# First Strassen pair's weight sums issued ahead of the norm, and the spatial norm's weight and bias applied after the mixing product

## The chip, the cores and the metric

The kernel runs on 1 core of a Trainium2 chip. The metric is device time in microseconds (us) of one execution. The engines are named as the profile names them: PE (TensorE matmul), PEld (its weight load), DVE (VectorE), ACT (ScalarE), POOL (GpSimd), SP (SyncE, which issues DMAs). Each engine takes its instructions in the order in which they were issued to it; an instruction that waits for a semaphore holds all that stand behind it on the same engine.

## The reference

One inference step of a model of two layers on 576 tokens (512 of a prompt, 64 new ones), width 1024, all in float32. Layer 0 mixes tokens with attention and a gated recurrence, layer 1 with chunked spatial gating; behind each mixer stands a gated feed-forward network (FFN) of inner width 2816 with a short causal convolution. After each of these four parts comes `x = layer_norm(alpha * x + f(x))`. What the change touches of it:

```
def layer_norm(x, g, b):
    mu = mean(x); var = mean((x - mu)**2)
    return (x - mu) * rsqrt(var + eps) * g + b

def odd_mixer(x, ...):                      # layer 1
    u, v = split(gelu(x @ w_in), 2)
    v = layer_norm(v, sgu_g, sgu_b)         # over the 1024 channels of a token
    ...
    v = sum over s <= t of sgu_w[group, t, s] * v[s] + sgu_bias[group, t]
    return (u * v) @ w_out                  # chunks of 128 tokens, 8 groups of 128 channels
```

The normalised v of the 64 new tokens is also an output of its own (output 14).

## The kernel before, in words

**Number format.** A float32 product is made of three passes of TensorE on a value's high part and low part: `xh*whi`, `xl*whi`, `xh*wlo` (a triplet, L419 to L421). A weight tile `raw` is split on the chip: ACT copies it into `whi` with rounding (L307), DVE subtracts `raw - whi` into `wlo` (L308). The residual stream is `x`, with channels on the partitions, in two halves of 288 tokens.

**FFN.** Function `ffn` makes the up-projection from 11 blocks of channel pairs. Blocks 0 and 1 are plain. From block 2 on, each is a Strassen pair: 7 products in place of 8, for which sums of token halves of x (`x_sums`, L1364 to L1381) and sums of weight halves are needed. The weight work of a pair (`pair_weights`) is: high and low part of two raw tiles; four sums of 128x512 on POOL, in place on the raw tiles, called s1, s3 (on the second tile) and s2, s4 (on the first) (L1263 to L1267); for each of the two summed tiles two ACT copies (L1276, L1277) and a DMA from POOL's queue (L1278) that adds the raw tile onto the negated high part, which gives the low part. A planner (class `Plan`, L70) puts this work, with costs and due times, into the queues; when a raw tile is used up, the load of a later unit is issued on SP (L1230).

**Start of an FFN.** At an FFN's start the norm of the residual is only half done. The first products, of the first token half (`sweep(us, 0, ...)`), run on PE while the second half ("half 1") is normalised by hooks that the sweep calls after so many of its steps: at step 13 `stats` (sums by PE at L554, a few small DVE instructions, the power on POOL at L564), at 15 `center` (mean spread by PE transposes at L571 into a PSUM bank; ACT copies it into `cs`, L578; 5 subtractions on DVE at L581, 3 on POOL at L583), at 17 and 20 `scale` (per channel block k: DVE L591, then ACT makes `xh` at L593, POOL the scaled x at L594, DVE `xl` at L603). At step 2 the hook `begin` (L1538 to L1541) splits the first Strassen pair's two plain operands. The rest of that pair's weight work is given to the planner behind the sweep, by `pair_weights(g2, begun=True)`. Then PE does the second token half of blocks 0 and 1 (`plain_second`, L1211 in the trace, as are all products of the planner), which needs `xh` and `xl` of half 1 for one k after the other.

**Spatial gating.** v is computed token-major by `v_sweep` (L824 to L826) into `vo` (four tiles of 128 tokens, one of 64, 1024 channels wide). Then DVE takes statistics (L1671, L1672), POOL the power (L1674), ACT normalises the five tiles (L1678), and each tile is multiplied by `gB` (DVE, L1679) and gets `bB` added (POOL for tiles 0 to 2, DVE for 3 and the sample tile 4, L1680). Meanwhile PE computes three of the u units (4, 5, 6; L419 to L421). Next `mix_sample` multiplies the sample tile by the masked spatial weights `wsT` (L1688), DVE adds the spatial bias `sB` (L1689), and `mix(g)` does the same for one group of the prompt (L1694, L1696) and multiplies by u (L1698); mixes 0 and 1 come at once, mix 2 between the halves of u unit 7, mixes 3 to 7 inside the loop over k of the output projection, whose products need their results `hh` (ACT, L1700) and `hl` (DVE, L1707). The mixing products have plain float32 operands, and the trace shows two records for each matmul of the code. `psmain` holds 6 PSUM banks named `mm` and 2 named `aux`; `auxbank()` hands out the two `aux` banks in turn, and the next user of a bank waits until the last reader of it is done.

Of the kernel before, what the change touches and what calls it, by code (L numbers as in the profile page):

```python
# [19 lines left out]
FT = mybir.dt.float32  # L20
# [5 lines left out]
D = 1024  # L26
# [145 lines left out]
def stream_step(ctx, tc, I, O):  # L172
# [44 lines left out]
    def weight_list():  # L217
        w = I["w_in_e"]
        E = {}
        col = {"q": 0, "k": 512, "xb": 1544, "gb": 2056}  # L220
        for name in ("xb0", "xb1", "xb2", "xb3", "gb0", "gb1", "gb2", "gb3"):
            E[name] = wunit(w, 0, EC, col[name[:2]] + 128 * int(name[2]), 0, 8, "A")
        E["v"] = [vunit(w, EC, 1024, 2 * i, "A", 520) for i in range(4)]
        for name in ("q0", "k0", "q1", "k1", "q2", "k2", "q3", "k3"):
            E[name] = wunit(w, 0, EC, col[name[:-1]] + 128 * int(name[-1]), 0, 8, "A")
        E["out"] = [wunit(I["w_out_e"], 0, D, 128 * m, 0, 8, "A") for m in range(8)]
        Fs = []

        def ffn_units(layer):
            up, down = {}, {}  # L230
            w = I["ffn_w_up"]

            def src(j, s, slot):
                return (w, layer * D * 2 * DFF, 2 * DFF, s * DFF + 128 * j, 0, 8, slot)

            for j in range(2):
                up[j] = [wunit(*src(j, s, "B")) for s in range(2)]
            tmp = [Unit(None, None, 0) for _ in range(2)]
            units.extend(tmp)
            for j in range(2, NJ):  # L240
                up[j] = wpair(wsrc(*src(j, 0, None)), wsrc(*src(j, 1, None)), j)
            for c, (j0, j1) in enumerate(CHUNKS):
                for m in range(8):
                    u = down[c, m] = wsrc(I["ffn_w_down"], layer * DFF * D, D, 128 * m, j0, j1 - j0, None)
                    u.slots = [j % RING for j in range(j0, j1)]
                    if c == len(CHUNKS) - 1:
                        units.append(u)
            Fs.append((up, down, tmp))

        ffn_units(0)  # L250
        w = I["w_in_o"]
        Od = {}
        Od["u"] = {}
        for m in range(4):
            Od["u"][m] = wunit(w, 0, 2 * D, 128 * m, 0, 8, "A")
        Od["v"] = [[vunit(w, 2 * D, D + 512 * s, 2 * i, "A") for i in range(4)] for s in range(2)]
        for m in range(4, 8):
            Od["u"][m] = wunit(w, 0, 2 * D, 128 * m, 0, 8, "A")
        Od["out"] = [wunit(I["w_out_o"], 0, D, 128 * m, 0, 8, "A") for m in range(8)]
        ffn_units(1)  # L260
        return E, Fs, Od

# [207 lines left out]
    class Norm:  # L470
# [100 lines left out]
                PE.transpose(bk[:, t:t + n], self.st[half][:n, c + j:c + j + 1].to_broadcast([n, 128]), ident[:n, :n])  # L571
            return bk[:, :b - a]

        def center(self, half):
            a, b = self.halves[half]
            mu = self.spread(half, 0)
            ms = self.cs[half]
            ACT.activation(ms, mu, AF.Copy)  # L578
            for k in range(8):
                if k < 5:  # L580
                    DVE.tensor_sub(x[:, k, a:b], x[:, k, a:b], mu)  # L581
                else:
                    POOL.tensor_sub(x[:, k, a:b], x[:, k, a:b], ms)  # L583
# [592 lines left out]
    def ffn(layer, prev, norm):  # L1176
# [68 lines left out]
        def sl(j, q):  # L1245
            return ("S", j % 2, q, "h", 0), ("S", j % 2, q, "h", 1), ("S", j % 2, q, "l", 0), ("S", j % 2, q, "l", 1)

        def pair_weights(g, begun=False):
            j = g.j
            r1, r2 = rres(g.one), rres(g.two)  # L1250
            R = lambda e, c: (g.one if e == 1 else g.two).raw[:, c]
# [1 line left out]
            h0, h1, l0, l1 = sl(j, 0)  # L1253
            k0, _, m0, _ = sl(j, 1)
            al = slice(0, 1024)
            if not begun:
                plan.add("ACT", 1.05, lambda: ACT.activation(W(0)[0][:, al], R(1, al), AF.Copy), r1, (h0, h1), tag=f"a1hi{j}")
                plan.add("DVE", 1.22, lambda: DVE.tensor_sub(W(0)[1][:, al], R(1, al), W(0)[0][:, al]), r1 + (h0, h1),
                         (l0, l1), True, tag=f"a1lo{j}")
                plan.add("ACT", 0.62, lambda: ACT.activation(W(1)[0][:, a_], R(2, b_), AF.Copy), r2[1:], (k0,), tag=f"a2hi{j}")  # L1260
                plan.add("DVE", 0.69, lambda: DVE.tensor_sub(W(1)[1][:, a_], R(2, b_), W(1)[0][:, a_]), (r2[1], k0),  # L1261
                         (m0,), True, tag=f"a2lo{j}")
            plan.add("POOL", 1.3, lambda: POOL.tensor_add(R(2, b_), R(2, a_), R(2, b_)), r2, r2[1:], True, tag=f"s1_{j}")  # L1263
            plan.add("POOL", 1.3, lambda: POOL.tensor_sub(R(2, a_), R(1, a_), R(2, a_)), (r1[0], r2[0]), r2[:1], True, tag=f"s3_{j}")
            split_sums(g, 2, r2)
# [274 lines left out]
            DVE.tensor_sub(l2[:, a_], g2.two.raw[:, b_], h2[:, a_])  # L1540
            DVE.tensor_sub(l1[:, :1024], g2.one.raw[:, :1024], h1[:, :1024])  # L1541

        hooks[2] = begin
        sweep(us, 0, xh, xl, g_first, outer=True, hooks=hooks)
        retire(us)
        close_ln()
# [1 line left out]
        sum_tiles(tp)  # L1548
        loaded["dma"], loaded["freed"] = st["dma"], st["freed"]
        x_sums()  # L1550
        pair_weights(g2, begun=True)
        d_next()
        plain_second(0)
        base(0, 1)
# [77 lines left out]

    first_group([Od["u"][m] for m in range(4)], u_post, n2)
    vo = op.tile([128, 5, D], FT, name="vo")
    gB = op.tile([128, D], FT, name="gB")
    bB = op.tile([128, D], FT, name="bB")
    sB = op.tile([128, 8, 128], FT, name="sB")
    wsr = op.tile([128, 8, 128], FT, name="wsr")
    wsT = op.tile([128, 8, 128], FT, name="wsT")
    nc.sync.dma_start(wsr, dram(I["sgu_w"], 0, [[128, 128], [128 * 128, 8], [1, 128]]))  # L1640
    nc.sync.dma_start(gB, dram(I["sgu_g"], 0, [[0, 128], [1, D]]))
    nc.sync.dma_start(bB, dram(I["sgu_b"], 0, [[0, 128], [1, D]]))
    nc.sync.dma_start(sB, dram(I["sgu_bias"], 0, [[0, 128], [128, 8], [1, 128]]))
    up_mask = op.tile([128, 128], FT, name="up_mask")
    jo = op.tile([128, 128], I32, name="jo")
    POOL.iota(jo, pattern=[[1, 128]], base=0, channel_multiplier=-1)
# [26 lines left out]
    DVE.tensor_scalar(rsv, mv[:, :, 1], EPS, None, op0=OP.add)  # L1673
    POOL.tensor_tensor(rsv, rsv, nhalf[:, 0:5], op=OP.pow)  # L1674
    DVE.scalar_tensor_tensor(mv[:, :, 0], mv[:, :, 0], -1.0, rsv, op0=OP.mult, op1=OP.mult)
    for t in range(5):
        n = 128 if t < 4 else TS
        ACT.activation(vo[:n, t], vo[:n, t], AF.Identity, scale=rsv[:n, t:t + 1], bias=mv[:n, t, 0:1])  # L1678
        DVE.tensor_mul(vo[:n, t], vo[:n, t], gB[:n])  # L1679
        (POOL if t < 3 else DVE).tensor_add(vo[:n, t], vo[:n, t], bB[:n])  # L1680
    nc.sync.dma_start(dram(O[14], 0, [[D, TS], [1, D]]), vo[:TS, 4])

    ms = op.tile([128, 8, TS], FT, name="ms")

    def mix_sample():
        bk = mmbank().rearrange("p (g t) -> p g t", g=8)
        for g in range(8):
            PE.matmul(bk[:, g], vo[:TS, 4, 128 * g:128 * g + 128], wsT[:TS, g, :TS], start=True, stop=True)  # L1688
        DVE.tensor_add(ms, bk, sB[:, :, :TS])  # L1689

    def mix(g):
        bk = auxbank()
        for t in range(4):
            PE.matmul(bk[:, 128 * t:128 * t + 128], vo[:, t, 128 * g:128 * g + 128], wsT[:, g, :], start=True, stop=True)  # L1694
        mt = op.tile([128, T], FT, name="mt", bufs=3)
        DVE.tensor_add(mt[:, :TP].rearrange("p (n t) -> p n t", n=4), bk.rearrange("p (n t) -> p n t", n=4),  # L1696
                       sB[:, g, None, :].to_broadcast([128, 4, 128]))
        DVE.tensor_mul(mt[:, :TP], mt[:, :TP], x[:, g, :TP])  # L1698
        POOL.tensor_mul(mt[:, TP:], ms[:, g], x[:, g, TP:])
        ACT.activation(hh[:, g, :], mt, AF.Copy)  # L1700
        mts[g] = mt
        mix_low(g - 1)
        POOL.tensor_add(x[:, g, :], xh[:, g, :].bitcast(FT), xl[:, g, :].bitcast(FT))
# [174 lines left out]
```

## Time and profile before

| | us |
|---|---|
| median of 3 runs | 1285.21 |
| lowest and highest run | 1285.07, 1285.76 |
| the profiled execution's own time | 1287.51 |
| its span, first to last instruction | 1285.5 |

The rows further down come from the one profiled execution. A row of the timeline gives start, duration, engine, line, operation and tiles; "x8" joins 8 instructions of a kind, and the brackets name the engine's idle time before it and what ended it. PE is busy for 96% of the span, DVE 79%, ACT 52%, POOL 46%; the mean granted clock of TensorE is 0.985 of full speed. Times in the kernel's course, in us of the span: layer 0's mixer to about 265, its FFN to about 660, layer 1's mixer to about 860, its FFN to the end.

### The profile page before, as it was taken

What the parts mean: (1) busy time and instruction counts of PE and PEld (TensorE: products, weight loads), DVE (VectorE), ACT (ScalarE), POOL (GpSimd) and SP (SyncE); (2) the same over time, 40 slices, a digit from 0 to 9 for tenths busy, and PEclk for the clock granted to TensorE, in tenths of its full rate; (3) what the DMA queues carried; (4) which work ended last, traced back from release to release, by engine and by line L of the source; (5) the groups of instructions that cost most, each with busy time, mean ns of one, the idle gap of its engine ahead of it and who ended that gap; (6) DMA issues with size and microseconds to landing.
All of it is one profiled execution on the core that took longest, in us unless ns stands there. A gap on an engine that the chain in (4) does not pass through costs nothing.

```text
span 1285.5 us, 23770 instructions
## 1 busy us (share of the span) xinstructions
PE 1238.7 (96%) x9111; PEld 1198.7 (93%) x9111; DVE 1010.2 (79%) x1874; ACT 664.6 (52%) x1062; POOL 592.6 (46%) x650
## 2 busy tenths in 40 slices
PE   8999999998999999999999998999899999999995
PEld 7999887998999999999989788998899999999995
DVE  4647686789998899878875238888899898888877
ACT  4553554348655656556444233347565556655542
POOL 3223132486455556555054005765645546555313
PEclk9999999999999999999989998999999999999998
DMA  8415320306755768766521422214657667956512
GB/s 224 133 34 164 100 92 27 104 1 146 177 138 146 168 144 195 162 143 144 144 69 38 160 66 62 63 54 100 141 121 179 147 144 178 196 127 162 134 47 75
DMA packets 204566, 155.78 MB, mean 121 GB/s; under 512 B 6524, under 2 KB 187036, under 8 KB 204452
## 3 DMA queue, kind: packets, MB, share of 16 engines
q1 hardware_dynamic: 192324, 111.96, 30.2%
q0 software_dynamic: 12128, 42.30, 18.5%
q8 instruction: 72, 1.18, 0.4%
q14 instruction: 42, 0.34, 0.1%
HBM read 107.07 MB, written 5.22 MB: 87 GB/s over the span
## 4 chain that ended last, share of the span: by engine, by line
PE 70%; DVE 13%; issue 9%; ACT 3%; POOL 3%; DMA 2%; DVEq 0%; SPq 0%; POOLq 0%; ACTq 0%
PE mm L1211 33%; PE aux L1211 17%; PE mm L419 4%; PE mm L420 4%; PE mm L421 4%; POOL x L594 2%; DMA wloB<-raw 1%; DVE raw L1364 1%; DVE wloA L308 1%; PE o L1103 1%; PE aux L554 1%; DVE vo L1679 1%; DMA raw<-in_w_in_e_dram 1%; ACT whiA L307 1%; PE mm L772 1%
## 5 line engine op out<-in xcount | busy, mean ns | idle before, releaser
L1324 DVE SCALAR_TENSOR_TENSOR y<-hb,vecF,y 128x578 f32<-128x578 f32 x176 | 166.3, 974 | 4.8 <-ACT y L1314 3.4
L308 DVE TENSOR_TENSOR wloA<-raw,whiA 128x1024 fp32r<-128x1024 f32 (+2 forms) x54 | 65.6, 1232 | 97.3 <-ACT whiA L307 97.3
L1211 PE MATMUL mm<-xh,wloB 128*128 128x288 f32 x384 | 113.4, 295 | 0.0
L1211 PE MATMUL mm<-xl,whiB 128*128 128x288 f32 x384 | 113.4, 295 | 0.0
L1211 PE MATMUL mm<-xh,whiB 128*128 128x288 f32 x384 | 113.4, 295 | 0.0
L419 PE MATMUL mm<-xh,whiA 128*128 128x288 f32 (+2 forms) x320 | 96.5, 302 | 3.9 <-ACT xh L650 3.9
L1211 PE MATMUL mm<-xh,whiA 128*128 128x288 f32 x320 | 94.8, 296 | 5.2 <-ACT xh L1379 3.6
L1263 POOL TENSOR_TENSOR raw<-raw 128x512 f32<-128x512 f32 x40 | 59.2, 1479 | 87.0 <-DVE wloA L1261 35.9
L421 PE MATMUL mm<-xh,wloA 128*128 128x288 f32 (+2 forms) x320 | 95.0, 297 | 1.5 <-DVE wloA L308 1.5
L1211 PE MATMUL mm<-xl,whiA 128*128 128x288 f32 x320 | 94.9, 297 | 1.0 <-DVE xl L1381 1.0
L420 PE MATMUL mm<-xl,whiA 128*128 128x288 f32 (+2 forms) x320 | 95.3, 298 | 0.4 <-DVE xl L651 0.4
L1338 POOL COPY stage<-hb 128x4 f32<-128x4 f32 x88 | 50.8, 677 | 95.5 <-DVE hb L1483 69.8
L1211 PE MATMUL mm<-xh,wloA 128*128 128x288 f32 x320 | 94.5, 295 | 0.0
L1447 DVE TENSOR_TENSOR x<-x,aux 128x288 f32<-128x288 f32 x160 | 71.4, 448 | 23.5 <-PE aux L1211 22.4
L1314 ACT ACTIVATE y<-hb,vecF 128x578 f32<-128x578 f32 x88 | 74.5, 864 | 29.5 <-DVE hb L1483 20.7
L307 ACT ACTIVATE whiA<-raw 128x1024 fp32r<-128x1024 f32 (+2 forms) x54 | 54.4, 1022 | 62.5 <-PE mm L826 44.4
L1211 PE MATMUL aux<-hh,wloA 128*128 128x288 f32 x272 | 80.8, 297 | 1.5 <-DVE wloA L1422 1.5
L1211 PE MATMUL aux<-hh,whiA 128*128 128x288 f32 x272 | 81.1, 298 | 0.2
L1211 PE MATMUL aux<-hl,whiA 128*128 128x288 f32 x272 | 80.8, 297 | 0.0
L1211 PE MATMUL aux<-hl,whiB 128*128 128x288 f32 x272 | 80.4, 296 | 0.0
L1211 PE MATMUL aux<-hh,wloB 128*128 128x288 f32 x272 | 80.4, 295 | 0.0
L1211 PE MATMUL aux<-hh,whiB 128*128 128x288 f32 x272 | 80.3, 295 | 0.0
(435 smaller groups left out, 4682.0 us busy)
## 6 DMA issues: line engine op xcount, KB each, us to landing
raw<-in_ffn_w_up_dram SPq DMA_DIRECT2D x88, 512.0 KB
wloA<-raw POOLq DMA_DIRECT2D x40, 512.0 KB, 5.0
wloB<-raw POOLq DMA_DIRECT2D x40, 512.0 KB, 4.9
draw<-in_ffn_w_down_dram SPq DMA_DIRECT2D x80, 192.0 KB
raw<-in_w_in_o_dram SPq DMA_DIRECT2D x16, 512.0 KB
raw<-in_w_in_e_dram SPq DMA_DIRECT2D x14, 512.0 KB
raw<-in_ffn_w_down_dram SPq DMA_DIRECT2D x16, 320.0 KB
raw<-in_w_out_e_dram SPq DMA_DIRECT2D x8, 512.0 KB
```

The lines of the kernel that those rows point to most:

```text
L307: ACT.activation(u.hi[:, c], u.raw[:, c], AF.Copy)
L308: DVE.tensor_sub(u.lo[:, c], u.raw[:, c], u.hi[:, c])
L419: PE.matmul(o, wh, h[:, k, a:b], start=first, stop=False)
L420: PE.matmul(o, wh, l[:, k, a:b], start=False, stop=False)
L421: PE.matmul(o, wl, h[:, k, a:b], start=False, stop=last)
L594: POOL.tensor_scalar(xk, xk, g, bb, op0=OP.mult, op1=OP.add)
L1211: PE.matmul(bank[key][:, :w], lhs(), rhs(), start=first, stop=stop)
L1263: plan.add("POOL", 1.3, lambda: POOL.tensor_add(R(2, b_), R(2, a_), R(2, b_)), r2, r2[1:], True, tag=f"s1_{j}")
L1314: plan.add("ACT", 0.86, lambda: ACT.activation(y, t[:, 2:580], AF.Identity, scale=V[:, 88 + ct:89 + ct], bias=V[:, 132 + ct:133 + ct]), hr ...
L1324: plan.add("DVE", 0.82, lambda q=q, y=y, t=t, ct=ct: DVE.scalar_tensor_tensor(y, t[:, q:q + 578], V[:, 44 * q + ct:44 * q + ct + 1], y, op ...
L1338: plan.add("POOL", 0.4, lambda s=s, t=t: POOL.tensor_copy(stage[:, :, s * NJ + j].rearrange("p (a b) -> p a b", a=2), t[:, 448:580].rearra ...
L1447: DVE.tensor_add(xm, xm, bank[key][:, :H2])
```

## The change

**Part one, both FFNs.** The first Strassen pair's sums, high parts and accumulating DMAs leave the planner and become hooks of the sweep, written out by hand: at step 3 the sums s1 and s3, at 6 the two ACT copies of the second tile (`parts(2)`), at 13 the stats, then the second tile's DMA (`rest(2)`) and the sums s2 and s4, at 15 the centre, now with all 8 subtractions on DVE, then `parts(3)`, `rest(3)` and the release of both raw tiles. In the list of loads, the two empty units that stand for the temporary buffers move from ahead of pair 2 to behind it, so that the next pair's raw tiles are asked for earlier.

**Part two, spatial gating.** `vo` stays without g and b, but for the sample tile's copy that goes to output 14. g and b come as 16 rows of 128 (`gbr`), a PE transpose makes columns of them, which DVE copies into `gbc` (b times 1024). Since g and b belong to a channel and the mixing sums over tokens, b's share of the result is b times the column sum of `wsT`: two matmuls with a column of 1/1024 give these sums, and 8 DVE instructions add them, times b, to `sB`. g is applied where the bias is added.

```diff
@@ load order
             tmp = [Unit(None, None, 0) for _ in range(2)]
-            units.extend(tmp)
             for j in range(2, NJ):
                 up[j] = wpair(wsrc(*src(j, 0, None)), wsrc(*src(j, 1, None)), j)
+                if j == 2:
+                    units.extend(tmp)
@@ Norm.center
-        def center(self, half):
+        def center(self, half, on_vector=5):
...
-                if k < 5:
+                if k < on_vector:
@@ ffn
-        hooks[2] = begin
+        def sums(q):
+            r1, r2 = g2.one.raw, g2.two.raw
+            if q == 2:
+                POOL.tensor_add(r2[:, b_], r2[:, a_], r2[:, b_])
+                POOL.tensor_sub(r2[:, a_], r1[:, a_], r2[:, a_])
+            else:
+                POOL.tensor_sub(r1[:, a_], r2[:, b_], r1[:, a_])
+                POOL.tensor_sub(r1[:, b_], r1[:, b_], r1[:, a_])
+
+        def parts(q):
+            hi, lo = (t[:, :1024] for t in S[0][q])
+            r = (g2.two if q == 2 else g2.one).raw[:, :1024]
+            ACT.activation(hi, r, AF.Copy)
+            ACT.activation(lo, r, AF.Copy, scale=-1.0)
+
+        def rest(q):
+            POOL.dma_start(S[0][q][1][:, :1024], (g2.two if q == 2 else g2.one).raw[:, :1024], accum_op=OP.add)
+
+        def middle():
+            prev.stats(1)
+            rest(2)
+            sums(3)
+
+        def end():
+            prev.center(1, 8)
+            parts(3)
+            rest(3)
+            free_raw(2)
+
+        hooks.update({2: begin, 3: lambda: sums(2), 6: lambda: parts(2), 13: middle, 15: end})
         sweep(us, 0, xh, xl, g_first, outer=True, hooks=hooks)
...
         x_sums()
-        pair_weights(g2, begun=True)
         d_next()
@@ spatial gating
-    for t in range(5):
+    for t in (4, 0, 1, 2, 3):
         n = 128 if t < 4 else TS
         ACT.activation(vo[:n, t], vo[:n, t], AF.Identity, scale=rsv[:n, t:t + 1], bias=mv[:n, t, 0:1])
-        DVE.tensor_mul(vo[:n, t], vo[:n, t], gB[:n])
-        (POOL if t < 3 else DVE).tensor_add(vo[:n, t], vo[:n, t], bB[:n])
-    nc.sync.dma_start(dram(O[14], 0, [[D, TS], [1, D]]), vo[:TS, 4])
+    DVE.tensor_mul(gB, vo[:TS, 4], gB)
+    DVE.tensor_add(gB, gB, bB)
+    nc.sync.dma_start(dram(O[14], 0, [[D, TS], [1, D]]), gB)
+    bk = auxbank()
+    PE.transpose(bk[:, :16], gbr, ident[:16, :16])
+    DVE.tensor_copy(gbc[:, 0:8], bk[:, 0:8])
+    DVE.tensor_scalar(gbc[:, 8:16], bk[:, 8:16], float(D), None, op0=OP.mult)
+    for g0 in (0, 4):
+        bk = auxbank()
+        PE.matmul(bk, mone[:, 0:1].to_broadcast([128, 128]), wsT[:, g0:g0 + 4].rearrange("p g t -> p (g t)"),
+                  start=True, stop=True)
+        for g in range(4):
+            DVE.scalar_tensor_tensor(sB[:, g0 + g], bk[:, 128 * g:128 * g + 128], gbc[:, 8 + g0 + g:9 + g0 + g], sB[:, g0 + g],
+                                     op0=OP.mult, op1=OP.add)
...
-        DVE.tensor_add(ms, bk, sB[:, :, :TS])
+        DVE.tensor_mul(ms, bk, gbc[:, 0:8, None].to_broadcast([128, 8, TS]))
+        DVE.tensor_add(ms, ms, sB[:, :, :TS])
...
-        DVE.tensor_add(mt[:, :TP].rearrange("p (n t) -> p n t", n=4), bk.rearrange("p (n t) -> p n t", n=4),
-                       sB[:, g, None, :].to_broadcast([128, 4, 128]))
+        DVE.scalar_tensor_tensor(mt[:, :TP].rearrange("p (n t) -> p n t", n=4), bk.rearrange("p (n t) -> p n t", n=4),
+                                 gbc[:, g:g + 1], sB[:, g, None, :].to_broadcast([128, 4, 128]), op0=OP.mult, op1=OP.add)
```

How instructions move on the engines, at the places that matter (names with A or B are the tiles' buffers).

PE in the changed kernel, right behind the last product of `v_sweep` (L827), with the semaphores that an instruction waits for; `mone` holds 1/1024:

```order
L827 MATMUL mm<-whiA,xl 64x512
L1717 MATMUL aux<-ident,gbr 128x16 [waits DMAHW4_49,DMAHW3_49,DVE_49]
L1722 MATMUL aux<-wsT,mone 128x512 [waits DVE_49]
L1722 MATMUL aux<-wsT,mone 128x512 [waits DVE_49,PE_49]
L420 MATMUL mm<-xh,whiA 128x288 [waits Activation_49]
```

The three new matmuls stand between `v_sweep` and u unit 4 (L420), which before followed it directly. The three take the two `aux` banks in turn, so the second column sum writes the bank of the transpose.

DVE before, from the last small instruction of the statistics to the first that reads mixed values:

```order
L1675 SCALAR_TENSOR_TENSOR mv<-mv,rsv 128x5
L1679 TENSOR_TENSOR vo<-vo,gB 128x1024 x4
L1680 TENSOR_TENSOR vo<-vo,bB 128x1024
L1679 TENSOR_TENSOR vo<-vo,gB 64x1024
L1680 TENSOR_TENSOR vo<-vo,bB 64x1024
L308 TENSOR_TENSOR wloA<-raw,whiA 128x1024 x3
L1689 TENSOR_TENSOR ms<-mm,sB 128x512
```

The same place in the changed kernel:

```order
L1707 SCALAR_TENSOR_TENSOR mv<-mv,rsv 128x5
L1711 TENSOR_TENSOR gB<-vo,gB 64x1024
L1712 TENSOR_TENSOR gB<-gB,bB 64x1024
L1718 COPY gbc<-aux 128x8
L1719 TENSOR_SCALAR gbc<-aux 128x8
L1725 SCALAR_TENSOR_TENSOR sB<-aux,gbc,sB 128x128 x8
L309 TENSOR_TENSOR wloA<-raw,whiA 128x1024 x3
L1733 TENSOR_TENSOR ms<-mm,gbc 128x512
```

The wide multiplications and additions are gone; the two reads of the transpose's bank (L1718, L1719) stand behind the statistics and behind the sample tile's two instructions.

ACT at the start of an FFN in the changed kernel, from the end of `begin` to the making of `xh` of half 1 (before, only `cs` stood between the first and the last of these rows):

```order
L1539 ACTIVATE whiA<-raw 128x1024
L1555 ACTIVATE whiA<-raw 128x1024
L1556 ACTIVATE wloA<-raw 128x1024
L579 ACTIVATE cs_2684<-aux 128x288
L1555 ACTIVATE whiA<-raw 128x1024
L1556 ACTIVATE wloA<-raw 128x1024
L594 ACTIVATE xh<-x,vec 128x288 x8
```

POOL at the same place, changed:

```order
L1546 TENSOR_TENSOR raw<-raw 128x512
L1547 TENSOR_TENSOR raw<-raw 128x512
L565 TENSOR_TENSOR sb<-sb,nhalf 96x3
L1559 DMA wloA<-raw 128x1024
L1549 TENSOR_TENSOR raw<-raw 128x512
L1550 TENSOR_TENSOR raw<-raw 128x512
L1559 DMA wloA<-raw 128x1024
L595 TENSOR_SCALAR x<-x,vec 128x288 x8
```

Before, the power (L564), three subtractions of the centre (L583) and the eight scalings (L594) came first, and the four sums and two DMAs behind them. Now two sums stand ahead of the power, and both DMAs and two sums ahead of the scalings.

## Rows read from the trace of the kernel before

**Rows 1.** Timeline of PE in spatial gating: start, us, engine, line.

```profile
759.00 0.29 PE L419 MATMUL mm<-xh,whiA 128*128 128x288 f32 x1
...
783.51 3.64 PE L1688 MATMUL mm<-wsT,vo 64*128 64x64 f32 x16 [5.26 <-DVE vo L1680]
787.08 3.78 PE L1694 MATMUL aux<-wsT,vo 128*128 128x128 f32 x16
...
794.74 1.05 PE L1694 MATMUL aux<-wsT,vo 128*128 128x128 f32 x8
```

**Rows 2.** Timeline of DVE in spatial gating: the sample tile's product with g.

```profile
780.90 1.21 DVE L1679 TENSOR_TENSOR vo<-vo,gB 64x1024 f32<-64x1024 f32 x1
```

**Rows 3.** Timeline of ACT in spatial gating.

```profile
767.34 5.78 ACT L1678 ACTIVATE vo<-vo,mv,rsv 128x1024 f32<-128x1024 f32 x5 [4.68 <-DVE mv L1675]
```

**Rows 4.** PE, line L772: float32 products of 289 and 290 columns in layer 0.

```profile
L772 PE MATMUL mm<-xc,wax x32: 404/407/512, 54.2 to 62.2; 128*128 128x290 f32 x16, 128*128 128x289 f32 x16
```

**Rows 5.** Stretches: length, busy PE, PEld, DVE, ACT, POOL, granted clock, DMA share, GB/s.

```profile
304.50:308.00 3.50, 3.50 (x16) 3.45 (x16) 3.31 (x6) 3.17 (x5) 1.96 (x3) 0.51 0.93 253
783.50:792.60 9.10, 9.09 (x41) 8.98 (x42) 7.01 (x8) 0.69 (x1) 2.17 (x3) 0.50 0.74 202
262.00:345.00 83.00, 77.91 (x571) 76.42 (x571) 75.80 (x130) 54.99 (x87) 56.66 (x67) 0.98 0.47 105
855.00:945.00 90.00, 82.59 (x603) 80.69 (x602) 78.94 (x139) 55.26 (x89) 56.09 (x70) 0.98 0.47 103
```

**Rows 6.** PE's waits between 262 and 345 us, layer 0's FFN.

```profile
PE mm L1211 <- ACT xh L1379: 2.5, 1, 2.5
PE mm L1211 <- DMA wloB<-raw: 1.2, 2, 0.7
```

**Rows 7.** PE's waits between 855 and 945 us, layer 1's FFN.

```profile
PE mm L1211 <- DMA wloB<-raw: 3.1, 2, 1.9
PE mm L1211 <- ACT y L1477: 1.6, 1, 1.6
PE mm L1211 <- ACT xh L1379: 1.1, 1, 1.1
```

**Rows 8.** Timeline of ACT at the start of layer 0's FFN.

```profile
270.39 1.04 ACT L1539 ACTIVATE whiA<-raw 128x1024 fp32r<-128x1024 f32 x1
273.31 0.41 ACT L578 ACTIVATE cs<-aux 128x288 f32<-128x288 f32 x1 [1.88 <-PE aux L571]
276.06 2.89 ACT L593 ACTIVATE xh<-x,vec 128x288 fp32r<-128x288 f32 x5 [2.34 <-DVE x L591]
```

**Rows 9.** Timeline of POOL at the same place.

```profile
269.79 1.63 POOL L1524 COPY hb<-vecF 128x2 f32<-128x2 f32 x4
273.23 0.86 POOL L564 TENSOR_TENSOR sb<-sb,nhalf 96x3 f32<-96x3 f32 x1 [1.80 <-DVE sb L563]
...
276.80 6.61 POOL L594 TENSOR_SCALAR x<-x,vec 128x288 f32<-128x288 f32 x8 [0.39 <-ACT xh L593]
283.37 1.29 POOL L1263 TENSOR_TENSOR raw<-raw 128x512 f32<-128x512 f32 x1
...
290.90 0.96 POOL L1278 DMA_DIRECT2D wloA<-raw  x1 [2.98 <-ACT wloA L1277]
```

**Rows 10.** Timeline of DVE at the same place.

```profile
271.46 1.23 DVE L1541 TENSOR_TENSOR wloA<-raw,whiA 128x1024 fp32r<-128x1024 f32 x1
...
283.44 1.53 DVE L603 TENSOR_TENSOR xl<-x,xh 128x288 fp32r<-128x288 f32 x1 [0.41 <-POOL x L594]
284.90 3.63 DVE L1364 TENSOR_TENSOR raw<-x 128x576 f32<-128x576 f32 x2
...
290.05 1.42 DVE L1364 TENSOR_TENSOR raw<-x,raw 128x576 f32<-128x576 f32 x2
```

**Rows 11.** Timeline of PE: first product of `plain_second`, first of `x_sum3`'s.

```profile
280.47 0.30 PE L1211 MATMUL mm<-xh,whiB 128*128 128x288 f32 x1
...
303.44 0.40 PE L1211 MATMUL mm<-xh,whiA 128*128 128x288 f32 x1 [2.51 <-ACT xh L1379]
```

More of the change, by code (lines that the diff above doesn't have):

```diff
@@ L1246, in sl, with pair_weights @@
             return ("S", j % 2, q, "h", 0), ("S", j % 2, q, "h", 1), ("S", j % 2, q, "l", 0), ("S", j % 2, q, "l", 1)
-        def pair_weights(g, begun=False):
+        def pair_weights(g):
             j = g.j
@@ L1255, in pair_weights @@
             al = slice(0, 1024)
[L1256 to L1262, printed above, removed]
+            plan.add("ACT", 1.05, lambda: ACT.activation(W(0)[0][:, al], R(1, al), AF.Copy), r1, (h0, h1), tag=f"a1hi{j}")
+            plan.add("DVE", 1.22, lambda: DVE.tensor_sub(W(0)[1][:, al], R(1, al), W(0)[0][:, al]), r1 + (h0, h1),
+                     (l0, l1), True, tag=f"a1lo{j}")
+            plan.add("ACT", 0.62, lambda: ACT.activation(W(1)[0][:, a_], R(2, b_), AF.Copy), r2[1:], (k0,), tag=f"a2hi{j}")
+            plan.add("DVE", 0.69, lambda: DVE.tensor_sub(W(1)[1][:, a_], R(2, b_), W(1)[0][:, a_]), (r2[1], k0),
+                     (m0,), True, tag=f"a2lo{j}")
             plan.add("POOL", 1.3, lambda: POOL.tensor_add(R(2, b_), R(2, a_), R(2, b_)), r2, r2[1:], True, tag=f"s1_{j}")
@@ L1634, in stream_step @@
     vo = op.tile([128, 5, D], FT, name="vo")
-    gB = op.tile([128, D], FT, name="gB")
-    bB = op.tile([128, D], FT, name="bB")
+    gB = op.tile([TS, D], FT, name="gB")
+    bB = op.tile([TS, D], FT, name="bB")
+    gbr = op.tile([16, 128], FT, name="gbr")
+    gbc = op.tile([128, 16], FT, name="gbc")
     sB = op.tile([128, 8, 128], FT, name="sB")
@@ L1640, in stream_step @@
     nc.sync.dma_start(wsr, dram(I["sgu_w"], 0, [[128, 128], [128 * 128, 8], [1, 128]]))
-    nc.sync.dma_start(gB, dram(I["sgu_g"], 0, [[0, 128], [1, D]]))
-    nc.sync.dma_start(bB, dram(I["sgu_b"], 0, [[0, 128], [1, D]]))
+    nc.sync.dma_start(gbr[0:8], dram(I["sgu_g"], 0, [[128, 8], [1, 128]]))
+    nc.sync.dma_start(gbr[8:16], dram(I["sgu_b"], 0, [[128, 8], [1, 128]]))
     nc.sync.dma_start(sB, dram(I["sgu_bias"], 0, [[0, 128], [128, 8], [1, 128]]))
+    nc.sync.dma_start(gB, dram(I["sgu_g"], 0, [[0, TS], [1, D]]))
+    nc.sync.dma_start(bB, dram(I["sgu_b"], 0, [[0, TS], [1, D]]))
     up_mask = op.tile([128, 128], FT, name="up_mask")
```

## The prediction

> **What bounds the kernel now.** I read PE's waits first, then the timelines around the two changed places engine by engine, then the granted clock there. A wait counts where PE itself stands still, since PE is at work for nearly the whole span. Around the change it stands still in two kinds of places.
>
> In spatial gating PE finishes u units 4 to 6 and waits 5.26 us for the last addition of `bB` on DVE [rows 1]. The reader should also see what follows: 9.1 us at a granted clock of 0.50, the lower of TensorE's two levels, 1.2 in place of 2.4 GHz [rows 5]. Half of such a stretch is lost, 4.55 us, so the wait costs about 9.8 us in all. That is what part two can win.
>
> At the start of each FFN PE's idle time is 83.00 - 77.91 = 5.1 us of a stretch in layer 0 and 90.00 - 82.59 = 7.4 us in layer 1 [rows 5]. In layer 0 the large ones are 2.5 us for `xh` (L1379) and 1.2 us for the accumulated low parts `wloB` [rows 6]; in layer 1 they are 3.1 us for `wloB`, 1.6 us for `y` and 1.1 us for `xh` [rows 7]. Behind the 2.5 us come 3.5 us at clock 0.51 [rows 5], which cost another 1.75. That is what part one can win.
>
> **Part two, spatial gating.** Removed: wide products and sums on DVE and POOL. Their place is covered by PE's u4 to u6, except for the 5.26 us above. Added on PE: a transpose of 16 columns and two column sums of 512 columns, all ahead of u4. The price of a sum: 16 float32 products of 290 columns in the code (32 records) take 54.2 to 62.2 us, so 0.5 each [rows 4]; 512 columns make 0.9. The transpose has no row; between nothing and 0.5 I take 0.1, as it is so narrow.
>
> The step that decides is the second column sum. There are two `aux` banks; the transpose has one, the first sum the other, so the second sum writes the transpose's bank and waits until DVE has read it. On DVE those reads stand behind the statistics and behind the sample tile's product and sum, which wait for ACT's normalisation. PE takes its instructions in order, so u4, which is ready, waits too. By the rows:
> - PE is free at 759.00 [rows 1]; transpose and first sum bring it to 760.0.
> - ACT begins to normalise at 767.34 and needs 5.78 / 5 = 1.16 for a tile [rows 3]; the sample tile now comes first and is ready at 768.5.
> - DVE: product 1.21 [rows 2], sum of the same shape the same, to 770.9; the two reads of 8 columns, a hundredth of that width, at most 0.2 each: 771.3.
> - PE idles from 760.0 to 771.3, 11.3 us, then the second sum to 772.2.
> - u4 to u6 take what they took from 759.00 to the start of the old wait, 783.51 - 5.26 = 778.25: 19.25 us, to 791.45.
> - After an idle time PE runs at the low level for a while. The FFN's dense triplets lost 1.75 so, the small mixing products 4.55. The work here is the triplets' kind, but the idle time is the longest of all; I take 2.6, nearer the triplets' row. `mix_sample` then starts at 794.05.
> - No wait remains there and the clock is full. From `mix_sample` to the third mix it took 794.74 - 783.51 = 11.2 [rows 1]; less 4.55 that is 6.7. The third mix starts at 800.75 in place of 794.74.
>
> So part two costs **+6.0 us** (5.2 with a clock loss of 1.75, 8.0 with 4.55): an old wait of 9.8 leaves, a new one of 11.3 + 2.6 and 1.9 of products come. From there on DVE has one instruction in place of one for each mix, so the lag stays.
>
> The Trainium skill (TensorE: Matmul & The Clock Gate, Part 1) says that the throttled state is the default and that activity releases it. By that rule the dense triplets, which leave no gap, would end the low level as in the FFN's row, and the time would be 0.9 us below mine; the mixing row, which stays low for 9.1 us with PE busy throughout, speaks against so plain a reading.
>
> **Part one, each FFN.** Removed from behind the sweep: four ACT copies, four POOL sums and two DMAs for the first pair. They now stand inside the sweep, under PE products, so as work they cost nothing; but they stand ahead of the last norm's half 1 on ACT and POOL, and PE's `plain_second` needs that half from 280.47 on [rows 11]. Worked out for layer 0:
> - POOL is free at 271.4 (269.79 + 1.63) and makes s1 and s3 at 1.29 each [rows 9]: to 274.0, if DVE's split of 1.23 at 271.46 [rows 10] doesn't hold it up, else to 275.3. That one holds up the other is seen at 284.90, where two sums of x take DVE 3.63 beside POOL's sums, and 1.42 at 290.05 [rows 10].
> - ACT's two copies, 1.04 each [rows 8], wait for them: to 276.1 or 277.4. `cs`, which stands behind them, comes 2.8 to 4.1 late, and DVE's centre waits for it. DVE has eight subtractions now, which delays nothing, as the next waits are longer.
> - POOL issues the DMA (0.96), then s2 and s4: to 279.7 or 281.0; ACT's next two copies to 281.8 or 283.1. Only then can ACT make the first `xh`, in place of 276.06 [rows 8]: 5.7 to 7.0 late.
> - POOL issues the second DMA at that point, then scales eight blocks in 6.61 [rows 9]: to 289.3 or 290.6. The last `xl` follows some 0.5 later, in place of 284.97 [rows 10].
> - `plain_second` goes through k in order; five of its 48 products are left when the last `xl` comes. At the 19.25 / 144 = 0.134 us of the triplets above it ended at 286.9 and now ends at 290.5 or 291.8: +3.6 to +4.9, and I take **+4.3**, the middle, since both engines start within 0.1 us of each other.
>
> The Trainium skill (SBUF — State Buffer, Who interferes with whom) says that the first to issue holds the shared ports and the other blocks wholly. By that POOL, 0.04 us ahead, would not be slowed, the lag would be 3.6 in each layer, and the time 1.4 us below mine.
>
> Against the lag: the pair's low parts are in SBUF long before they are due, and the next raw tiles are asked for earlier, so the `wloB` waits go; the wait for `xh` (L1379) takes up lag, if its chain (copies on ACT, sums on DVE) is not late as well. Its start is as late as PE, but four copies, 4 x 1.04 = 4.2, have left ACT in front of it, and DVE's loss of 2.2 beside POOL's sums goes. I count it as taken up. The clock loss of 1.75 moves from behind that wait to behind the new one, net nothing. Layer 0: 4.3 - 2.5 - 1.2 = **+0.6**. Layer 1, taken with the same lag: 4.3 - 1.1 - 3.1 - 1.6 = **-1.5**. Bounds for a layer: none of the waits given back, +4.3; all given back and no lag, -5.1 and -7.4.
>
> **Sum.** 6.0 + 0.6 - 1.5 = +5.1. The profiled span of 1285.5 becomes 1290.6, that execution's own 1287.51 becomes 1292.6, and the median of the runs, which lies 2.3 below it, 1285.21 + 5.1 = **1290.3**.
>
> **The rivals.**
> 1. Faster: PE doesn't stop at the second column sum, because the bank is free (the reads of the transpose come before 760.9, ahead of the statistics). Then u4 to u6 end at 759.0 + 1.9 + 19.25 = 780.15, the third mix starts at 786.85, 7.9 early; with -0.9 of the FFNs 1276.4. The listed order of PE and DVE speaks against it; nothing in the rows supports it.
> 2. Faster: the weight work fits in front of the norm after all. It decides if the first `xh` of half 1 is there before about 278.6, two microseconds (ACT, POOL, DVE for one block) ahead of 280.47. Then all waits and both clock losses go, 5.1 + 7.4 + 3.5 = 16.0, and 6.0 stays: 1275.2. ACT would have to finish its copies 3 us sooner than the POOL rows allow.
> 3. No change: the FFNs give back 5 to 7 us in all, as their lag is smaller than mine or more of the small waits go, and cancel spatial gating: near 1285.
> 4. Slower still: the chain to `xh` (L1379) is as late as PE, so nothing is taken up, and +4.3 stays in each layer: 6.0 + 8.6 = 14.6, 1299.8.
>
> **How the numbers follow.** The forecast has 0.68: its FFN sum may be off by 3 us and its clock loss by 2, so its own range is 1286 to 1295.5. Rival 1 has 0.06, rival 2 0.06, rival 3 0.11, rival 4 0.09. A measurement here tells about 0.2%, 2.6 us, from no change. Faster: rivals 1 and 2 and a little of 3, 0.14. Same: most of 3 and the low edge of the forecast, 0.13. Slower: the rest, 0.73. The range that leaves out 2 in 10 takes in the forecast, most of rival 3 and the low part of rival 4: 1283.5 to 1297.
>
> **What would show it.** Right: PE's list of waits has one for the second column sum (L1722) of 10 to 12 us released by DVE, none at the mix; ACT's first `xh` of half 1 stands behind the second pair of copies at about 282 to 283; PE waits in `plain_second` by about 4 us in each layer; the `wloB` waits of the first pair are gone. Wrong: u4 directly behind `v_sweep`; `plain_second` without a wait; or a clock that stays low far past 4 us behind the new wait.

## The result and the profile after

The changed kernel takes 1298.62 us (median of 4 runs, 1297.84 to 1299.83) where the kernel before takes 1285.14: a ratio of 1.0109 with a 95% interval of 1.0097 to 1.0121, or 13.5 us. The forecast was +5.1 us and a range that ended at 1297. The profiled execution took 1299.33, with a span of 1297.5.

Where does PE stand still now? Its largest waits over the whole run (engine, line, releaser: us in total, times, longest):

```profile
PE aux L1722 <- DVE gbc L1719: 11.0, 1, 11.0
PE mm L1212 <- DVE xl L604: 5.1, 2, 2.5
PE mm L1212 <- ACT y L1477: 4.5, 2, 3.2
...
PE aux L572 <- POOL sb L565: 3.9, 2, 1.9
...
PE mm L1212 <- ACT xh L594: 1.4, 1, 1.4
```

The first is in spatial gating and stands in place of the 5.26 us before the mix [rows 1]. The others lie at the start of the two FFNs, in place of the waits for `xh` and `wloB` [rows 6, 7]. L572 is the norm's spread by PE transposes; it is its second use, the spread of the power, that waits here. L1477 is ACT's copy of P1, one of a Strassen pair's seven products, out of its PSUM bank.

**Spatial gating.** PE's timeline in the changed kernel:

```profile
763.31 0.23 PE L1717 MATMUL aux<-ident,gbr 16*128 16x16 f32 x1
763.47 1.12 PE L1722 MATMUL aux<-wsT,mone 128*128 128x512 f32 x2
775.58 2.04 PE L1722 MATMUL aux<-wsT,mone 128*128 128x512 f32 x2 [10.99 <-DVE gbc L1719]
...
798.46 2.00 PE L1732 MATMUL mm<-wsT,vo 64*128 64x64 f32 x16
...
805.47 1.05 PE L1739 MATMUL aux<-wsT,vo 128*128 128x128 f32 x8
```

and DVE's, from the sample tile's product to the two reads of the transpose's bank:

```profile
772.82 1.22 DVE L1711 TENSOR_TENSOR gB<-vo,gB 64x1024 f32<-64x1024 f32 x1 [1.37 <-ACT vo L1710]
774.07 1.22 DVE L1712 TENSOR_TENSOR gB<-gB,bB 64x1024 f32<-64x1024 f32 x1
775.21 0.15 DVE L1718 COPY gbc<-aux 128x8 f32<-128x8 f32 x1
775.29 0.15 DVE L1719 TENSOR_SCALAR gbc<-aux 128x8 f32<-128x8 f32 x1
```

From the transpose to the third mix PE needs 805.47 - 763.31 = 42.2 us; before, from u4's start to the same mix, 794.74 - 759.00 = 35.7 [rows 1]. Gating lost 6.4 us.

**The FFNs.** I count PE's matmuls from the first one behind the norm's stats in both traces and compare when the n-th starts; the difference is PE's lag. Behind `plain_second` (the 150th) it is 7.9 us in layer 0 and 9.0 in layer 1; at the 350th, near the end of the first pair's window (the products under which the planner puts this pair's work), 4.9 and -0.1, and from there it stays within 0.4 of that to the FFN's end. So against this one execution of the kernel before, layer 0 lost 4.9 us and layer 1 nothing. How far one execution can be trusted is seen in the two kernels further down that change gating alone: with the FFNs as before, their lag at the 350th is -0.2 and -0.2 in layer 0, but -2.8 and -0.7 in layer 1. Layer 1's figures hold to 2 or 3 us only. POOL and ACT at the start of layer 0's FFN, in the order that the change gave them:

```profile
270.18 2.36 POOL L1546 TENSOR_TENSOR raw<-raw 128x512 f32<-128x512 f32 x1
272.62 1.26 POOL L1547 TENSOR_TENSOR raw<-raw 128x512 f32<-128x512 f32 x1
273.85 0.86 POOL L565 TENSOR_TENSOR sb<-sb,nhalf 96x3 f32<-96x3 f32 x1
...
282.74 0.87 POOL L1559 DMA_DIRECT2D wloA<-raw  x1 [2.59 <-ACT xh L594]
283.38 2.67 POOL L595 TENSOR_SCALAR x<-x,vec 128x288 f32<-128x288 f32 x4
286.76 3.47 POOL L595 TENSOR_SCALAR x<-x,vec 128x288 f32<-128x288 f32 x4 [0.70 <-ACT xh L594]
```

```profile
280.18 1.06 ACT L1555 ACTIVATE whiA<-raw 128x1024 fp32r<-128x1024 f32 x1 [3.96 <-POOL raw L1550]
281.15 1.04 ACT L1556 ACTIVATE wloA<-raw 128x1024 fp32r<-128x1024 f32 x1
282.09 2.17 ACT L594 ACTIVATE xh<-x,vec 128x288 fp32r<-128x288 f32 x4
286.03 2.86 ACT L594 ACTIVATE xh<-x,vec 128x288 fp32r<-128x288 f32 x4 [1.77 <-DVE x L592]
...
310.43 1.06 ACT L1277 ACTIVATE wloB<-raw 128x1024 fp32r<-128x1024 f32 x1 [1.60 <-POOL raw L1264]
311.39 1.04 ACT L1276 ACTIVATE whiB<-raw 128x1024 fp32r<-128x1024 f32 x1
312.33 0.39 ACT L1477 ACTIVATE y<-mm 128x288 f32<-128x288 f32 x1
```

The power (L565) ends at 274.7, behind s1 and s3; `xh` begins at 282.09 behind the second pair of copies. This execution reached the stats 1.2 us earlier than the one of the kernel before, so with 1.2 added, as 275.9 and 283.3, they are to be read against 274.1 and 276.06 there [rows 8, 9]. The granted clock (the figure before the DMA share) falls behind each of the waits:

```profile
775.60:779.00 3.40, 3.40 (x9) 2.36 (x10) 2.19 (x8) 1.72 (x2) 0.00 (x0) 0.50 0.38 82
...
276.00:280.00 4.00, 4.00 (x21) 4.00 (x20) 3.75 (x11) 0.22 (x1) 3.42 (x3) 0.57 0.55 104
286.00:290.00 4.00, 4.00 (x21) 4.00 (x20) 3.44 (x9) 3.62 (x8) 3.29 (x5) 0.57 0.19 37
313.00:316.50 3.50, 3.50 (x19) 3.50 (x19) 3.43 (x9) 1.46 (x2) 2.83 (x4) 0.63 0.69 131
```

### The profile page after: what moved, and what is told of

It reads as the page before. It is cut to its first block, busy times and chain, and to the rows that moved or that the text cites. A ratio compares the mean times of both kernels' runs of the same rounds, so it can differ in the third digit from the quotient of the medians.

```text
span 1297.5 us, 23785 instructions
## 1 busy us (share of the span) xinstructions
PE 1244.3 (96%) x9116; PEld 1203.5 (93%) x9116; DVE 990.9 (76%) x1886; ACT 664.7 (51%) x1062; POOL 578.5 (45%) x641
## 5 line engine op out<-in xcount | busy, mean ns | idle before, releaser
L1212 PE MATMUL mm<-xl,whiB 128*128 128x288 f32 x384 | 116.0, 302 | 5.1 <-DVE xl L604 5.1
L420 PE MATMUL mm<-xh,whiA 128*128 128x288 f32 (+2 forms) x320 | 97.8, 306 | 1.8 <-ACT xh L651 1.8
```

Source lines behind the costliest of these rows:

```text
L420: PE.matmul(o, wh, h[:, k, a:b], start=first, stop=False)
L1212: PE.matmul(bank[key][:, :w], lhs(), rhs(), start=first, stop=stop)
```

## The experiments

All were timed against runs of the kernel before on the same chip; the difference given is between the medians.

**Each part alone.** The diff's FFN hunks, and its gating hunks.

> The kernel before with part one alone (both FFNs), spatial gating as before. The theory drawn from the two traces (the lag of PE behind the norm's sums settles at +4.6 us in layer 0 and -0.3 in layer 1): +4.3 us, about 1289.4. If the whole loss were in spatial gating: within 1 us of before.

> The kernel before with part two alone. The theory (from the end of v_sweep to the third mix 42.2 in place of 35.7 us): +6.4 to +7.6 us, about 1292, with an 11 us wait of PE at the second column sum and none at the mix. If the two parts only cost time together: less than +3.

FFNs alone: 1290.78 against 1284.25, +6.5 us, ratio 1.0048 (1.0036 to 1.006). Gating alone: 1292.05, +7.8 us, 1.0062 (1.0049 to 1.0076), with the same 11.0 us wait. The two add up to 14.3 where both together showed 13.5, so within the noise they don't meet. The FFNs cost 1.7 us more than the changed kernel's lags make, 4.9 - 0.1, and more than the +4.3 expected; where this lies is not shown. This run's trace has a low stretch of the clock of 1.5 us ahead of layer 1's stats, which the changed kernel's has not (last section), but its lag in layer 1 is lower by as much, -1.7, so the two cancel. The lags are counted against a single execution of the kernel before, and a slow one of its kind (1287.51 where the median of its runs is 1285.21): the span of part one's profiled execution, 1289.4, is only 3.9 above that one's.

**Gating: the bank.** The changed kernel with the second column sum in another bank.

```diff
     for g0 in (0, 4):
-        bk = auxbank()
+        bk = auxbank() if g0 == 0 else mmbank()
         PE.matmul(bk, mone[:, 0:1].to_broadcast([128, 128]), ...
```

> The changed kernel with the second column sum in one of the mm banks; nothing else. The theory (PE stands still only for the transpose's bank): the 11 us wait goes, u unit 4 follows the sums, the third mix comes about 27.9 us after the end of v_sweep in place of 42.2, so some 14 us less: about 1284. Rival (the loss is in the added products, the clock or DVE's longer path to sB): a wait of PE of 5 us or more stays before or at the mix, and the time falls by less than 5 us.

> Part two alone with the second column sum in an mm bank; FFNs as before. The theory (without the wait for the bank part two saves the old wait at the mix and its low-clock stretch, 9.8 us, less 1.9 for the column sums and the transpose, less about 1 us of new waits in the output projection): 6 to 8 us less than before. Rival (PE only comes sooner to a later wait): within 2 us of before.

In the changed kernel: 1285.31, so 13.3 us less than without this edit (across chips; against before on its own chip +1.1, ratio 1.0008, 0.9998 to 1.0017). PE's timeline in it:

```profile
763.34 0.23 PE L1717 MATMUL aux<-ident,gbr 16*128 16x16 f32 x1
763.50 1.12 PE L1722 MATMUL aux<-wsT,mone 128*128 128x512 f32 x2
764.46 1.02 PE L1722 MATMUL mm<-wsT,mone 128*128 128x512 f32 x2
...
784.47 2.00 PE L1732 MATMUL mm<-wsT,vo 64*128 64x64 f32 x16
...
791.49 1.05 PE L1739 MATMUL aux<-wsT,vo 128*128 128x128 f32 x8
```

No wait is left at the sums or the mix, and the third mix comes 28.1 us behind the transpose in place of 42.2: the 11 us of waiting and the low stretch behind them were the bank's. With part two alone the same edit gives 1280.70 against 1284.86, -4.2 us, ratio 0.9965 (0.9952 to 0.9977), less than the 6 to 8 expected. Its third mix is 7.6 us early, as expected; 1.5 of it was lost again ahead of layer 1's norm, where this run's clock fell (last section), and 0.8 at waits for `hl` in the output projection, 1.5 in place of 0.7; the rest is open. The same edit is worth 5.5 us on top of part one (1285.31 against 1290.78), so 4.2 is not a fixed price.

**FFN: the norm first.** Part one, with s1 and s3 behind the power, and the copies and other sums behind `xh` and the scalings; the first tile's copies and DMA go to the planner.

```diff
         def middle():
-            prev.stats(1)
-            rest(2)
-            sums(3)
+            prev.center(1, 8)
+            sums(2)
         def end():
-            prev.center(1, 8)
-            parts(3)
-            rest(3)
-            free_raw(2)
-        hooks.update({2: begin, 3: lambda: sums(2), 6: lambda: parts(2), 13: middle, 15: end})
+            parts(2)
+            rest(2)
+            sums(3)
+        hooks.update({2: begin, 15: middle, 21: end})
...
+        split_sums(g2, 3, rres(g2.one))
+        freed(2)
         x_sums()
```

> Part one alone, but the first pair's sums and copies issued behind the norm's own work on ACT and POOL: s1 and s3 behind the power, the copies and the other sums behind xh and the scalings, the first tile's copies and DMA left to the planner. Load order as in the change. The theory (the lag in FFN comes from the norm of half 1 standing behind that work): no wait of PE at the second spread, none above 1 us in plain_second, and 3 to 6 us less than part one alone in layer 0, 5 to 9 in layer 1, so 1275 to 1282. Rival (the lag comes from the new load order or the planner's new order): within 2 us of part one alone.

1289.68 against 1284.25: +5.4 us, ratio 1.004 (1.0026 to 1.0053), only 1.1 less than part one alone, which is not clear of noise and short of the 1275 to 1282 expected. The lag behind `plain_second` did go, to 0.0 and -0.3 us, but by the 350th product it was 1.8 in layer 0 and -0.1 in layer 1 (part one alone: 5.0 and -1.7). PE's waits in layer 0, 266 to 350 us:

```profile
PE mm L1212 <- ACT y L1477: 1.8, 1, 1.8
PE mm L1212 <- DVE hl L1367: 1.7, 2, 1.4
```

L1367 makes the low part of a sum of x. So the norm's lag was real, but PE, no longer late, lost time in the window behind it, where part one alone had taken lag up. P1's copy (L1477) stands behind the next pair's copies on ACT, which wait for POOL (the changed kernel's rows at 310.43 to 312.33). In layer 1 that wait is 3.3 us here and 1.3 in the changed kernel.

**Four runs through the planner.** P1's copy made to go first by a dependency (`after=`) of the next pair's copies: in the norm-first kernel, with the x sums' copies ahead as well, and in part one alone. Then the load order of the change alone, in the kernel before. Last, both parts together: the first of these FFNs, and gating with the second column sum in an `mm` bank.

```diff
+            after = list(after) + [p1_copy[i] for i in [j - 1] if j == 3]
-            plan.add("ACT", 1.06, ..., r, h, tag=f"h{q}_{j}")
+            plan.add("ACT", 1.06, ..., r, h, after=after, tag=f"h{q}_{j}")
```

> The norm-first kernel with two more things ahead on ACT: the copies of the first x sums (L1365) ahead of the first tile's copies, and P1's copy (L1477) of the first pair ahead of the second pair's copies, which wait for POOL. The theory (with the norm out of the way, what is left of the loss in the FFNs is ACT standing at copies whose sums POOL has not made, while PE waits for L1477 and L1367): the waits of 1.8 and 3.3 us for L1477 and of 1.4 for L1367 go, with their low-clock stretches, 5 to 9 us less than norm-first, 1281 to 1285. Rival (PE only comes sooner to the next thing that is late, wloB or xh): within 2 us of norm-first.

> Part one alone, with P1's copy (L1477) of the first pair ahead of the second pair's copies on ACT; the norm's half 1 still stands behind the weight sums. The theory (two losses in series, the norm's lag and the wait for L1477): PE's 3.2 us wait for L1477 in layer 0 and its 1.6 in layer 1 go with their low-clock stretches, 3 to 6 us less than part one alone, about 1286. Rival (the wait for L1477 only covers something as late behind it): within 2 us of part one alone.

> The kernel before with the new order of loads alone (the two empty units behind pair 2, both raw pairs released in that order). The theory (the wloB waits of before, 1.2 and 3.1 us, come from the late raw tiles of the next pair): part of them goes, 0 to 4 us less than before. Rival (the new load order is what costs in the FFNs): 3 us or more above before.

> Both parts with what the runs so far suggest: gating with the second column sum in an mm bank, the norm first, the x sums' and P1's copies first. The theory (the costs are these three waits and add up): the gain of the last column-sum run over part two alone kernel, -6 to -8 us against before in gating, and the FFN result of the run with sums and P1 first: 1274 to 1280. Rival (the FFN's gain and gating's are both taken up elsewhere): 1283 or more.

All missed: 1304.59, 1313.22, 1318.32 and 1297.79 against 1285.46 (ratios 1.0139, 1.0215, 1.0255, 1.0095). In the first two the first window behaved as the theory said: at the 350th product of layer 0 the lag is -1.1 and 2.9. The loss comes later, 7.5 us between the 450th and the 750th product in the first of them. The load-order run has 5.3 at the 350th and 15.9 at the 750th. There PE waits for the down-projection's weights, between 345 and 400 us of the load-order run:

```profile
PE aux L1212 <- DVE wloB L1422: 2.1, 2, 1.5
PE aux L1212 <- ACT whiB L1417: 2.0, 1, 2.0
PE aux L1212 <- ACT whiA L1417: 1.6, 1, 1.6
PE aux L1212 <- DVE wloA L1422: 1.2, 2, 1.0
```

where before had a single such wait of 0.7 from 345 to 430. The planner orders the whole FFN from its estimates; a change of one input moved work in windows far behind it. So these runs say nothing on their edits as such, and the load order's own share in the changed kernel stays open, since it could not be changed without a new plan. It does not force the loss, though: the kernels of the next table have the same load order, and the last of them is faster than before.

**The same exchanges in the finished order.** The planner left as it is, its result edited before it is issued:

```diff
     def emit(self):
-        for i in self.order():
+        o, tag = self.order(), lambda i: self.ops[i][5]
+        for late, first in ((('h3_2', 'n3_2', 'acc3_2'), 't1hi'), (('h2_3', 'n2_3', 'acc2_3'), 'p1_2')):
+            at = max(k for k, i in enumerate(o) if tag(i) == first)
+            late = [i for i in o[:at] if tag(i) in late]
+            o = [i for i in o[:at] if i not in late] + [o[at]] + late + o[at + 1:]
+        for i in o:
```

> The norm-first kernel with P1's copy (L1477) moved ahead of the second pair's copies, and the x sums' first copies ahead of the first tile's copies, by exchanging places in the finished order, so that the planner's order is the same everywhere else. The theory (with the norm's lag gone, ACT's order in the first window is the rest of the loss in the FFNs, and the losses of the two runs before came from the planner ordering later windows anew): PE's position after the first window as in the run with sums and P1 first (2 us earlier than norm-first in layer 0, 3 in layer 1) and flat from there, so about 5 us less than norm-first, 1283 to 1286. Rival (ACT's order costs as such): 5 us or more above norm-first, as there.

> Part one alone with P1's copy moved ahead of the second pair's copies in the finished order, nothing else. The theory (the planner's new order of later windows made the run with P1's copy first slow): no loss of 5 us or more; the lag after the first window 0 to 4 us less than in part one alone in layer 0, so 1286 to 1291. Rival (that copy's place as such costs): 1300 or more.

> The norm-first kernel with P1's copy alone moved ahead of the second pair's copies in the finished order; the first tile's copies stay ahead of the x sums' copies. The theory (P1's copy is the larger of the two): PE's lag at the end of the first window about 1 us below norm-first in layer 0, the wait of 1.4 us for L1367 still there, 1284 to 1288. Rival (the x sums' place was the whole gain): within 1 us of norm-first. If P1's copy was all of it: 1282 to 1283.

| kernel, FFNs only | us against before | ratio (95%) | lag layer 0, 150th / 350th | lag layer 1 |
|---|---|---|---|---|
| part one as it is | +6.5 | 1.0036 to 1.0060 | 8.0 / 5.0 | 6.4 / -1.7 |
| norm first | +5.4 | 1.0026 to 1.0053 | 0.0 / 1.8 | -0.3 / -0.1 |
| P1's copy exchanged | +4.3 | 1.0021 to 1.0046 | 8.0 / 2.2 | 6.4 / -1.7 |
| norm first, P1's copy exchanged | +0.9 | 0.9996 to 1.0013 | -0.1 / 0.5 | -0.3 / -2.3 |
| norm first, both exchanged | -2.3 | 0.9974 to 0.9991 | 0.0 / -1.2 | -0.3 / -2.3 |

Either cure alone gains 1 or 2 us, both 5.6, and the x sums' place 3 more (these rows come from three chips, each against before on its own). That both gain 2.3 more than the two alone is not shown: the intervals of the four rows make some 3 us of doubt, and in layer 0's lag at the 350th it is the other way, 3.2 and 2.8 alone, 4.5 together. The lags stay flat behind the first window, so the order behind it, and not the place of the copy as such, was what the planner's runs had spoilt: P1's copy ahead in part one is 1313.22 through the planner and 1289.16 in the finished order. One thing I had wrong: the wait for P1's copy does not go. It is 2.0 us in layer 0 of the best FFN kernel, now because the copy itself waits for the tile that it writes:

```profile
306.48 0.41 ACT L1482 ACTIVATE y<-mm 128x288 f32<-128x288 f32 x1 [2.06 <-DVE hl L1339]
```

**The power first.** Part one, with the stats, and so the norm's power, ahead of s1 and s3 on POOL; no other engine's order changes.

```diff
             prev.stats(1)
+            sums(2)
+            parts(2)
             rest(2)
...
-        hooks.update({2: begin, 3: lambda: sums(2), 6: lambda: parts(2), 13: middle, 15: end})
+        hooks.update({2: begin, 13: middle, 15: end})
```

> Part one alone with the norm's power ahead of s1 and s3 on POOL; no other engine's order changes. Theory A (the lag in plain_second is set by when the last xl of half 1 is there, and the wait at the second spread is nested in it): that wait goes, the wait in plain_second grows by as much, the lag behind plain_second stays 7 to 9 us in layer 0, and the time stays within 1.5 us of part one alone. Theory B (the wait at the second spread and its low-clock stretch, 3.3 us in layer 0, add to the lag): the lag falls to 4 to 5 us, the time by 2 us or more.

1294.64 against 1284.31, +10.3, ratio 1.0075 (1.0061 to 1.0089): slower than part one alone, by more than theory A allowed (A: within 1.5 us; on different chips +10.3 against +6.5). PE's waits at the start of layer 0's FFN:

```profile
284.15 0.61 PE L1212 MATMUL mm<-xh,whiB 128*128 128x288 f32 x1 [4.93 <-ACT xh L594]
...
287.09 0.61 PE L1212 MATMUL mm<-xl,whiB 128*128 128x288 f32 x1 [2.32 <-DVE xl L604]
```

The wait at the second spread is gone and the lag behind `plain_second` is 10.1 us, where part one alone has 8.0. So theory B falls: that wait was nested in the later one. The lag follows the weight sums, which now start later, and with them `xh` and `xl`.

**The best of both.** Norm first with both exchanges, and the second column sum in an `mm` bank.

> Norm first with the exchanged places, and gating with the second column sum in an mm bank. If the parts add up: the result of the first kernel of this call and that of the last, less the kernel before, 1276 to 1281. Rival (one hides the other): 1284 or more.

1275.46 against 1284.86: ratio 0.9922 (0.9908 to 0.9936), 9.4 us faster than before and, across chips, 23 faster than the change. The two gains, 2.3 and 4.2, make 6.5, and the time lies a little below the range given. The traces of both parents have the low stretch of 1.5 us ahead of layer 1's stats (17.9 us between the stats of the two halves), this one has not (16.3, as before); the rest of the difference is not traced.

## Why the prediction was wrong

**Gating was right.** +6.0 forecast, 6.4 in the trace up to the third mix, 7.8 in the time of part two alone. By steps: from the transpose to the end of the wait 12.3 forecast, 775.58 - 763.31 = 12.3; the second sum and u4 to u6 22.8 forecast, 22.9; from `mix_sample` to the third mix 6.7 forecast, 7.0. The clock loss of 2.6 was right in size: the second sum took 2.04 in place of 1.0 and u4 to u6 20.8 in place of 19.25. The lag did not quite stay: from the third mix to the next norm's stats PE lost 1.3 more, 0.8 of it at two waits for `hl` in place of one. Taking the bank away took the loss away, so this cause is shown.

**The FFNs' sum was wrong.** -0.9 forecast for both, +6.5 measured for part one alone. The order of work was read rightly: the norm of half 1 is late because it stands behind the weight sums, and the run with the norm first removes the lag. Three terms failed.
- *"I take +4.3, the middle."* The lag was 7.9 and 9.0. It was worked out from the last `xl`, with five products left behind it. The last `xl` is there at 290.26 + 0.46 + 1.2 (the shift between the executions) = 291.9 in the time of before, where 289.8 to 291.1 were worked out, but PE does not wait for it: 21 of the 48 products are still to come. PE's only wait in layer 0's `plain_second` is for the first `xl`:

```profile
285.69 0.40 PE L1212 MATMUL mm<-xl,whiB 128*128 128x288 f32 x1 [2.53 <-DVE xl L604]
```

  In the time of before that is 286.9, and the product stood at 280.6 there, one behind the first of `plain_second` [rows 11]: 6.3 late. The low stretch behind the wait (286 to 290) makes 1.6 more, together 7.9. The first `xl` itself took 1.37 us where the later ones take 0.46, beside POOL's scalings; that these held it up is likely, but no run shows it:

```profile
284.26 1.37 DVE L604 TENSOR_TENSOR xl<-x,xh 128x288 fp32r<-128x288 f32 x1 [3.55 <-POOL x L595]
...
290.26 0.46 DVE L604 TENSOR_TENSOR xl<-x,xh 128x288 fp32r<-128x288 f32 x1 [0.41 <-POOL x L595]
```

- *"The clock loss of 1.75 moves from behind that wait to behind the new one, net nothing."* There are two low stretches, 276 to 280 behind the wait at the second spread and 286 to 290 behind the one for `xl`, each 4 us at 0.57, 1.7 lost in each. I had left out the wait at the second spread, 1.9 us; the run with the power first shows that it does not add of itself, since PE would have waited for `xl` the longer. The second stretch adds, and behind the new wait for P1's copy comes a third, 3.5 us at 0.63, 1.3 lost: about 2.9 in place of the 1.75.
- *Layer 0: 4.3 - 2.5 - 1.2 = +0.6.* The two waits went, as forecast. But a new one of 3.2 us for P1's copy came, and layer 0 ended at +4.9. I had looked at the waits that the change would remove, and not at the new order in which the planner, without the first pair's work, puts ACT's copies. Before, P1's copy stood ahead of the next pair's copies:

```profile
307.54 0.40 ACT L1477 ACTIVATE y<-mm 128x288 f32<-128x288 f32 x1
...
310.56 1.06 ACT L1277 ACTIVATE wloB<-raw 128x1024 fp32r<-128x1024 f32 x1 [1.89 <-POOL raw L1264]
```

  In layer 1, where -1.5 was forecast, the lag of 9.0 was taken up wholly in this trace, and a wait of 1.3 for P1's copy stayed. As layer 1 differs by up to 2.8 us between executions with the same FFN, its share of the +6.5 stays open.

Rival 4 named 1299.8, near the measured time, but by another cause: it kept 4.3 in each layer because nothing would be taken up, while in fact the lag was twice that and was taken up by 3.0 us in layer 0 and, in this trace, wholly in layer 1. That the number came near was luck.

On the ports, s1 took 2.36 us where such a sum took 1.29 [rows 9], and DVE's L1541, starting at the same 270.18, took its usual 1.23: POOL was the one held up, by 1.1 of those 1.23. The Trainium skill (SBUF — State Buffer, Who interferes with whom) has the loser block for the whole instruction; the rows agree. Its first to issue was not POOL here, on which the lower end of my lag rested: to the hundredth the two starts are the same, and the trace records DVE's 7 ns ahead.

## What to carry to other kernels

Before work is put ahead of something in an in-order queue, list what stands behind it there and when each is wanted; work that is free as work can still be dear by its place. The bank of a small helper product can hold up an engine as long as its slowest reader is late. A cure is to be judged by whether its own wait went, not by the time alone: the norm first took the whole lag of 8 us away and the time fell by 1 only, because the next window lost what it had been taking up. And where a planner orders the work from estimates, change its finished order for an experiment, not its input.

## What was not expected of the hardware

The same short wait of PE, 0.9 us for the norm's sums at the start of layer 1's FFN, was followed by full clock in some executions and by a low stretch in others: of the sixteen traces, one for each kernel, nine show the low stretch. The wait and the stretch behind it, in part two alone with the bank's edit:

```profile
PE aux L554 <- DVE s1r L539: 0.9, 1, 0.9
...
841.30:849.30 8.00, 8.00 (x56) 7.98 (x56) 5.66 (x17) 2.93 (x6) 5.49 (x7) 0.79 0.01 3
```

and in the changed kernel:

```profile
PE aux L555 <- DVE s1r L540: 0.9, 1, 0.9
...
859.00:867.00 8.00, 7.72 (x64) 7.71 (x65) 6.59 (x20) 3.33 (x7) 6.01 (x8) 1.00 0.24 69
```

0.79 over 8 us is 1.7 us lost, in a place that the edit doesn't touch. Whether it goes by the kernel or by the execution is not shown. It is as much as several of the effects studied here, and one reason to compare positions within a trace as well as whole times.
